# Second product of four gated MLPs by seven half-size products per block pair, in a tuned two-block transformer kernel

## The chip, the cores and the metric

The kernel runs on one core of a Trainium2 chip. The metric is the device time of one execution in microseconds (us), median over runs. The core has a matrix engine (TensorE, "PE" in the profile, its weight loads "PEld"), three elementwise engines (VectorE "DVE", ScalarE "ACT", GpSimd "POOL") and a queue of DMA issues (SyncE, "SP"). TensorE writes to 8 banks of PSUM, of 512 fp32 columns each; all else lies in one SBUF arena.

## The reference

512 tokens of width 1024 go through two layers of a first block and then through a second block. Each layer of the first block is: gated MLP, a mixer of three attentions, gated MLP. The change is about the four gated MLPs (`ffn1` and `ffn2` of both layers), and a little about two of the attentions:

```python
def swiglu(x, wg, wu, wd):                       # wg, wu: 1024 x 2816; wd: 2816 x 1024
    return (jax.nn.silu(x @ wg) * (x @ wu)) @ wd

x = x + 0.5 * swiglu(rmsnorm(x, ffn1_norm[l]), ffn1_wg[l], ffn1_wu[l], ffn1_wd[l])
```

The second block (two more mixers and 16 experts) is not touched. Everything is fp32. Each large product is made as three products of rounded operands (fp32r): with x = xh + xl and w = wh + wl it is wh·xh + wh·xl + wl·xh.

## The kernel before, in words

Activations lie feature-major: 128 features on the partitions, 512 tokens along the row. `ffn` (L783) has two halves. In the first, 11 groups `g` of 256 inner rows each make gate and up: per group 2 matrices x 2 tiles of 128 rows x 8 chunks of the 1024 inputs x 3 products, 96 matmuls of 512 columns. VectorE multiplies the gate sums by the norm's factor, ScalarE applies silu, VectorE multiplies by the up sums; the result of each 128-row tile is split into a rounded part `hh` and a rest `hl`, both kept for all 22 tiles. In the second half, 4 blocks `dp` of 256 output columns run over all 22 tiles: 22 x 2 x 3 = 132 matmuls of 512 columns each into two banks. Then VectorE scales each bank, adds it to the residual `x`, and `norm_prep` (L723) prepares the next norm: the scaled row, its rest, its square, the sum of squares.

Weights come as jobs of up to 128 x 1024 fp32 (`weights`, L666): a DMA into one of four raw buffers, a cast to fp32r (`copy`, L646: ScalarE or VectorE), and a subtraction in place for the rest (`tt`, L654: VectorE or GpSimd). Both helpers leave the engine open.

No order is written out by hand: `Recorder` (L77) first collects all operations with their dependencies, `schedule` (L296) then places them one by one on five engines with a table of assumed costs (`duration`, L518), chooses the engine of an operation with alternatives, gives PSUM banks to the products, and `search` keeps the best of nine tries. `emit` issues the result; each engine runs its list in that order. So all instructions have the line of `emit`, L500, and are told apart by shape. In the attentions some operands have 96 partitions (three parts of 32: `cqk`, `QP`, `KP`) and a few 64.

## Time and profile before

| | |
|---|---|
| runs of the kernel before | 2968.25 us median of 3 (2966.52 to 2971.15) |
| the profiled execution | 2972.06 us, span of its instructions 2970.3 us |
| granted TensorE clock, mean | 0.993 |
| TensorE busy | 2894.5 us, 97% of the span, 14909 matmuls |
| VectorE busy | 1669.2 us, 56% |
| ScalarE busy | 634.0 us, 21% |
| GpSimd busy | 279.2 us, 9% |

In the trace a matmul's record is longer than its turn on the engine, since matmuls are pipelined; the time of one in a row is the distance between two starts, or a stretch divided by its count. "Idle before" names what ended an engine's idle time. The arena is one tensor, so operations are named by their shape, and "bank" is PSUM.

### The profile page before, as it was taken

Reading aid. Unit: us, or ns where it says so; the run is one execution under the profiler, and the core shown is the slowest. Engines: PE = TensorE matmul, PEld = TensorE weight load, DVE = VectorE, ACT = ScalarE, POOL = GpSimd, SP = SyncE. Lnnn points to the kernel's source line nnn. Section 1 sums busy time; section 2 is a strip of 40 time slices with the busy share of each in tenths; the row PEclk is TensorE's granted clock in tenths of the full one; section 3 lists DMA queues with packets and bytes.
Section 4 is the critical chain, followed back from the end, with each engine's and each line's share of the span. In section 5 each row is a group of like instructions: output and inputs, shape, how many; then the busy total and the mean of one; then the engine's idle time right before and its main releaser. Section 6 shows DMA issues by size and latency. Waiting matters only on the chain.

```text
span 2970.3 us, 37457 instructions
## 1 busy us (share of the span) xinstructions
PE 2894.5 (97%) x14909; PEld 2192.1 (74%) x14909; DVE 1669.2 (56%) x3051; ACT 634.0 (21%) x1364; POOL 279.2 (9%) x279
## 2 busy tenths in 40 slices
PE   9999999999999999999999999999999999999998
PEld 7888877777888888888777778888777876444443
DVE  6554565886555455555658865555767783311212
ACT  3000133472000010001334721001222361100000
POOL 1000111211000010001112210000223120000000
PEclk9999999999999999999999999999999999999999
DMA  4333322102333333333221023333312356999999
GB/s 124 99 93 98 109 78 62 47 5 77 90 100 99 97 89 100 100 96 112 78 60 56 2 78 90 95 96 100 89 57 71 100 179 242 384 409 409 409 409 349
DMA packets 273139, 403.61 MB, mean 136 GB/s; under 512 B 34809, under 2 KB 210982, under 8 KB 272966
## 3 DMA queue, kind: packets, MB, share of 16 engines
q1 hardware_dynamic: 272806, 401.09, 40.1%
q8 instruction: 117, 1.92, 0.3%
q14 instruction: 56, 0.46, 0.0%
q0 software_dynamic: 160, 0.14, 0.0%
HBM read 399.09 MB, written 2.10 MB: 135 GB/s over the span
## 4 chain that ended last, share of the span: by engine, by line
PE 87%; DVE 8%; DMA 3%; issue 1%; ACT 1%; POOL 1%; SPq 0%; DVEq 0%; POOLq 0%; ACTq 0%
PE bank L500 87%; DVE arena L500 8%; DMA arena<-in_w_expert_up 1%; ACT arena L500 1%; DMA arena<-in_ffn_wd 1%; POOL arena L500 1%; DMA arena<-in_w_expert_down 0%; DMA arena<-in_x 0%; SPq L500 0%; DMA arena<-in_w_in 0%; DVEq L500 0%; DVEq L2189 0%; POOLq L500 0%; ACTq L500 0%
## 5 line engine op out<-in xcount | busy, mean ns | idle before, releaser
L500 PE MATMUL bank<-arena 128*128 128x512 f32 (+7 forms) x14909 | 2894.5, 383 | 71.7 <-DVE arena L500 40.5
L500 PEld LDWEIGHTS bank<-arena 128*128 128x128 f32 (+4 forms) x14681 | 2183.4, 176 | 751.9 <-issue 257.5
L500 DVE TENSOR_TENSOR arena<-arena 128x1024 fp32r<-128x1024 f32 (+11 forms) x889 | 689.5, 793 | 33.2 <-PE bank L500 9.1
L500 DVE CAST arena<-arena 128x1024 fp32r<-128x1024 f32 (+6 forms) x394 | 258.9, 658 | 629.4 <-PE bank L500 446.5
L500 POOL TENSOR_TENSOR arena<-arena 128x512 f32<-128x512 f32 (+13 forms) x159 | 206.6, 1306 | 1793.9 <-DVE arena L500 870.3
L500 ACT ACTIVATE arena<-arena 128x512 f32<-128x512 f32 (+4 forms) x313 | 189.2, 627 | 867.1 <-DVE arena L500 729.7
L500 ACT ACTIVATE arena<-bank,arena 128x256 f32<-128x256 f32 (+7 forms) x349 | 177.9, 534 | 452.5 <-PE bank L500 240.5
L500 DVE TENSOR_TENSOR arena<-arena,bank 128x512 f32<-128x512 f32 (+2 forms) x226 | 142.6, 668 | 103.4 <-PE bank L500 97.6
L500 ACT CAST arena<-arena 128x512 fp32r<-128x512 f32 (+3 forms) x94 | 74.5, 798 | 510.6 <-DVE arena L500 424.6
L500 ACT COPY arena<-bank 128x512 f32<-128x512 f32 (+5 forms) x194 | 102.8, 542 | 329.4 <-PE bank L500 324.6
L500 DVE TENSOR_TENSOR arena<-bank,arena 128x512 f32<-128x512 f32 (+3 forms) x207 | 135.2, 676 | 67.1 <-PE bank L500 50.0
L500 DVE SCALAR_TENSOR_TENSOR arena<-bank,arena 128x512 fp32r<-128x512 f32 (+5 forms) x71 | 46.6, 662 | 166.7 <-ACT arena L500 84.7
L500 DVE TENSOR_REDUCE arena<-bank 128x1 f32<-128x256 f32 (+3 forms) x208 | 97.5, 482 | 30.4 <-PE bank L500 27.2
L500 DVE TENSOR_SCALAR arena<-bank,arena 128x128 f32<-128x128 f32 (+5 forms) x88 | 32.4, 411 | 124.7 <-PE bank L500 124.4
L500 DVE TENSOR_SCALAR arena<-arena 128x512 f32<-128x512 f32 (+13 forms) x260 | 87.5, 358 | 17.4 <-ACT arena L500 12.3
L500 DVE COPY arena<-bank 128x512 f32<-128x512 f32 (+8 forms) x91 | 46.7, 514 | 85.2 <-PE bank L500 84.4
L500 DVE SCALAR_TENSOR_TENSOR arena<-arena 128x512 fp32r<-128x512 f32 (+8 forms) x162 | 86.5, 538 | 7.0 <-DMA arena<-in_attn_k_norm_w 4.3
L500 POOL TENSOR_SCALAR arena<-arena 128x512 f32<-128x512 f32 (+3 forms) x93 | 61.9, 668 | 295.2 <-DVE arena L500 259.7
L500 ACT CAST arena<-bank 128x512 fp32r<-128x512 f32 (+2 forms) x99 | 56.0, 577 | 94.8 <-PE bank L500 81.4
L500 ACT ACTIVATION_READ_ACCUMULATOR arena<-bank,arena 128x1 f32 x208 | 42.7, 205 | 0.0
L500 DVE RECIPROCAL arena<-arena 128x1 f32<-128x1 f32 (+2 forms) x249 | 38.0, 162 | 5.6 <-ACT arena L500 4.7
L500 PEld LDWEIGHTS <-arena 128*128 128x128 bf16 x228 | 21.4, 99 | 21.9 <-issue 15.1
(32 smaller groups left out, 157.6 us busy)
## 6 DMA issues: line engine op xcount, KB each, us to landing
arena<-in_w_expert_gate SPq DMA_DIRECT2D x64, 1024.0 KB
arena<-in_w_expert_up SPq DMA_DIRECT2D x64, 1024.0 KB
arena<-in_w_expert_down SPq DMA_DIRECT2D x62, 1024.0 KB
arena<-in_ffn_wg SPq DMA_DIRECT2D x88, 512.0 KB
arena<-in_ffn_wu SPq DMA_DIRECT2D x88, 512.0 KB
arena<-in_ffn_wd SPq DMA_DIRECT2D x80, 512.0 KB
arena<-in_w_in SPq DMA_DIRECT2D x36, 512.0 KB
arena<-in_w_in SPq DMA_DIRECT2D x32, 256.0 KB
```

Of the source, the lines that this page charges most:

```text
L500: last[i] = getattr(getattr(self.real, eng), m)(*a, **k).ins
```

## The change

The second product of each MLP is done by Strassen's scheme on blocks of 2 x 2: two tiles of inner rows times two tiles of output columns on the weights' side, two tiles of inner rows times two halves of the tokens on the activations' side. Where one pair of inner tiles and one column block took 12 matmuls of 512 columns, it now takes 7 products x 3 = 21 of 256 columns. For this

- `forms_b` replaces the split of a group's two tiles: 4 sums of 256 columns, and 7 forms (three plain, four sums) each with a rounded part and a rest;
- `forms_a` replaces `weights` for the second product's jobs: 4 sums of 256, then 7 forms with rounded part and rest, 1792 columns where there were 1024;
- `down` accumulates the seven products in four banks, and VectorE joins them by one copy and seven sums of 256 columns per column block; the scaling and the sum into `x` may now be done by GpSimd too;
- the inner rows are run in two chunks, groups 0 to 5 and 6 to 10, since all forms at once would not fit: six buffers for the activations' forms. So `x` is added to twice, and only the second chunk is followed by `norm_prep`.

In the attentions, operands of 96 or 64 partitions get 128, and GpSimd writes zeros into the rest (`blank`), once per buffer: 24 writes in all.

```diff
     def ffn(self, js, next_gain):
...
-                for f in range(2):
-                    t = hp.tile([128, T], F32, name="ht", tag="ht", bufs=3)
-                    h, lo = hh[:, 2 * g + f, :], hl[:, 2 * g + f, :]
-                    nc.vector.tensor_mul(t, ps[0][f], R)
-                    nc.scalar.activation(t, t, AF.Silu)
-                    nc.vector.tensor_mul(t, t, ps[1][f])
-                    self.copy(h, t)
-                    self.tt("tensor_sub", lo, t, f32(h))
...
-            for dp in range(4):
-                pds = [mmt() for _ in range(2)]
-                for gi, (f0, f1) in enumerate(self.fgs):
-                    wh, wl = self.weights(js["d"][dp][gi])
-                    for d in range(2):
-                        for f in range(f0, f1):
-                            self.mm3(pds[d], wh[:, f - f0, 128 * d:128 * d + 128], wl[:, f - f0, 128 * d:128 * d + 128],
-                                     hh[:, f, :], hl[:, f, :], f == 0, f == NF - 1)
...
+    CHUNKS = ((0, 6), (6, 11))
...
+                    B[g] = self.forms_b(hp, *ht)
+                if c:
+                    self.norm_end()
+                    self.norm2_begin() if next_gain == "two" else self.norm_begin(next_gain)
+                for dp in range(4):
+                    self.down(hp, mmt, js["d"][c][dp], B, g0, g1, dp, Rh)
+                    if c:
+                        for d in range(2):
+                            self.norm_prep(2 * dp + d)
+
+    def forms_b(self, hp, b1, b2):
...
+        hi, lo = (hp.tile([128, 7, 256], F32R, name=n, bufs=6) for n in ("bh", "bl"))
+        t = f32(lo[:, 3:7])
+        b11, b12, b21, b22 = b1[:, :256], b1[:, 256:], b2[:, :256], b2[:, 256:]
+        for n, (op, x, y) in enumerate((("tensor_sub", b12, b11), ("tensor_sub", b22, t[:, 0]), ("tensor_sub", b22, b12),
+                                        ("tensor_sub", t[:, 1], b21))):
+            self.tt(op, t[:, n], x, y)
+        w = lambda x: x.rearrange("p a b -> p (a b)")
+        for i, j, x in ((0, 1, b11), (1, 3, b2), (3, 7, w(t))):
+            h, o = w(hi[:, i:j]), w(lo[:, i:j])
+            self.copy(h, x)
+            self.tt("tensor_sub", o, x, f32(h))
+        return hi, lo
+
+    def forms_a(self, hp, j):
...
+        s = hp.tile([128, 1024], F32, name="sa", bufs=2)[:, :na * 512].rearrange("p (s a c) -> p s a c", s=4, a=na)
+        hi = hp.tile([128, 1792], F32R, name="ah", bufs=2)[:, :na * 896].rearrange("p (s a c) -> p s a c", s=7, a=na)
+        a11, a12, a21, a22 = v[:, :, 0, 0], v[:, :, 1, 0], v[:, :, 0, 1], v[:, :, 1, 1]
+        for i, (op, x, y) in enumerate((("tensor_add", a21, a22), ("tensor_sub", s[:, 0], a11), ("tensor_sub", a11, a21),
+                                        ("tensor_sub", a12, s[:, 1]))):
+            self.tt(op, s[:, i], x, y)
...
+        for h, x in ((hi[:, 0], a11), (hi[:, 1], a12), (hi[:, 2], a22), (w(hi[:, 3:7]), w(s))):
+            self.copy(h, x)
+            self.tt("tensor_sub", r32(x), x, f32(h))
...
+    def down(self, hp, mmt, jobs, B, g0, g1, dp, Rh):
...
+        ps = [mmt().rearrange("p (a b) -> p a b", a=2) for _ in range(4)]
+        for ga, gb, j in jobs:
+            ah, al = self.forms_a(hp, j)
+            for g in range(ga, gb):
+                bh, bl = B[g]
+                for m, n, q, e in self.PRODUCTS:
+                    w = ((ah, bh), (ah, bl), (al, bh))
+                    for i, (x, y) in enumerate(w):
+                        nc.tensor.matmul(ps[q][:, e], x(m, g - ga), y[:, n], start=g == g0 and i == 0 and e == 0,
+                                         stop=g == g1 - 1 and i == 2, skip_group_check=True)
+        (p1, p2), (p6, p7), (p5, p3), (p4, _) = [(p[:, 0], p[:, 1]) for p in ps]
...
+        self.copy(c1, p1)
+        nc.vector.tensor_add(y1[:, :256], c1, p2)
+        nc.vector.tensor_add(u2, c1, p6)
+        nc.vector.tensor_add(u3, u2, p7)
+        nc.vector.tensor_add(y1[:, 256:], u2, p5)
+        nc.vector.tensor_add(y1[:, 256:], y1[:, 256:], p3)
+        nc.vector.tensor_add(y2[:, 256:], u3, p5)
+        nc.vector.tensor_sub(y2[:, :256], u3, p4)
+        for d, y in enumerate((y1, y2)):
+            x = self.x[:, 2 * dp + d, :]
+            self.tt("tensor_mul", y, y, Rh)
+            self.tt("tensor_add", x, x, y)
...
-        KP = ap.tile([96, T], F32R, name="KP")
-        self.copy(KP, self.tr4(lambda c: self.three(hl[:, c]), pp))
+        KP = ap.tile([128, T], F32R, name="KP")
+        self.blank(KP, 96)
+        self.copy(KP[:96], self.tr4(lambda c: self.three(hl[:, c]), pp))
```

What the planner makes of it stands in the engines' lists. On TensorE, in the first MLP's second half, the list of before has products of 512 columns into two banks (arena_145 and arena_146 are the rounded part and the rest of the activations, arena_132 and arena_133 those of a job of weights):

```order
L500 MATMUL bank4_62<-arena_145,arena_132 128x512
L500 MATMUL bank2_60<-arena_146,arena_132 128x512
L500 MATMUL bank4_62<-arena_146,arena_132 128x512
L500 MATMUL bank2_60<-arena_145,arena_133 128x512
L500 MATMUL bank4_62<-arena_145,arena_133 128x512
```

Of the change, the start of the second chunk, behind the last gate and up products (arena_105 and arena_106 are the MLP's input, arena_147 and 148 the forms of a group's activations, arena_173 and 174 those of a job of weights):

```order
L500 MATMUL bank1_59<-arena_105,arena_130 128x512
L500 MATMUL bank1_59<-arena_106,arena_130 128x512
L500 MATMUL bank1_59<-arena_105,arena_135 128x512
L500 MATMUL bank5_63<-arena_147,arena_173 128x256
L500 MATMUL bank2_60<-arena_147,arena_173 128x256
L500 MATMUL bank4_62<-arena_147,arena_173 128x256
L500 MATMUL bank4_62<-arena_148,arena_173 128x256
L500 MATMUL bank4_62<-arena_147,arena_174 128x256
```

From there 420 products of 256 columns follow one another with none of 512 between them; in the first chunk the fourth column block alone is mixed with the next groups' gate and up products.

On VectorE, before, one column block's end and the weights of the next (arena_91 is `x`, 103, 105 and 106 the next norm's, 130 to 137 weights):

```order
L500 TENSOR_TENSOR arena_144<-bank1_59,arena_149 128x512
L500 TENSOR_TENSOR arena_147<-bank6_64,arena_149 128x512
L500 TENSOR_TENSOR arena_91<-arena_91,arena_144 128x512
L500 TENSOR_TENSOR arena_91<-arena_91,arena_147 128x512
L500 TENSOR_SCALAR arena_105<-arena_91,arena_98 128x512
L500 SCALAR_TENSOR_TENSOR arena_106<-arena_91,arena_98,arena_105 128x512
L500 CAST arena_132<-arena_136 128x1024
```

Of the change, at the same kind of place in the second chunk (arena_171 and 175 are the weights' sums, 177 and 178 forms, 179, 143 and 144 what is joined from the banks):

```order
L500 CAST arena_177<-arena_134 128x256
L500 CAST arena_173<-arena_132 128x256
L500 TENSOR_TENSOR arena_178<-arena_175,arena_177 128x1024
L500 TENSOR_TENSOR arena_135<-arena_134,arena_177 128x2x128
L500 TENSOR_TENSOR arena_179<-arena_179,bank0_58 128x256
L500 TENSOR_TENSOR arena_143<-arena_179,bank3_61 128x256
L500 TENSOR_TENSOR arena_135<-arena_134,arena_177 128x2x128
L500 TENSOR_TENSOR arena_143<-arena_179,bank5_63 128x256
L500 TENSOR_TENSOR arena_179<-arena_179,bank0_58 128x256
L500 TENSOR_TENSOR arena_171<-arena_124 128x128
```

The sums of banks and the forms of later jobs now stand between one another on one list. On GpSimd, before, these rows (the last is the mixer's) and one more sum into arena_103 and into `x` each are its arithmetic in the first MLP:

```order
L500 TENSOR_TENSOR arena_146<-arena_147,arena_145 128x512
L500 TENSOR_TENSOR arena_91<-arena_91,arena_147 128x512
L500 TENSOR_TENSOR arena_103<-arena_103,arena_107 128x512
L500 TENSOR_TENSOR arena_103<-arena_103,arena_108 128x512
L500 TENSOR_TENSOR arena_103<-arena_103,arena_107 128x512
L500 TENSOR_TENSOR arena_178<-arena_171,arena_177 128x576
```

Of the change, in the second chunk alone, 39 such operations, of which the first are:

```order
L500 TENSOR_TENSOR arena_166<-arena_143,arena_165 128x256
L500 TENSOR_TENSOR arena_171<-arena_171,arena_132 128x128
L500 TENSOR_TENSOR arena_171<-arena_132 128x128
L500 TENSOR_TENSOR arena_133<-arena_132,arena_173 128x128
L500 TENSOR_TENSOR arena_171<-arena_132,arena_171 128x128
L500 TENSOR_TENSOR arena_133<-arena_132,arena_173 128x128
L500 TENSOR_TENSOR arena_171<-arena_124 128x256
L500 TENSOR_TENSOR arena_135<-arena_134,arena_177 128x2x128 x2
```

GpSimd has taken over sums and rests that the weights' forms need, with 15 operations of 256 columns, 15 of 128 and 9 of 512 in that chunk.

## Rows read from the trace of the kernel before

**Rows 1.** The page, its first part: busy time by engine.
```profile
PE 2894.5 (97%) x14909; PEld 2192.1 (74%) x14909; DVE 1669.2 (56%) x3051; ACT 634.0 (21%) x1364; POOL 279.2 (9%) x279
```
**Rows 2.** The chain that ended last: start us, us, what, count.
```profile
PE 87%; DVE 8%; DMA 3%; issue 1%; ACT 1%; POOL 1%; SPq 0%; DVEq 0%; POOLq 0%; ACTq 0%
...
734.61 361.38 PE bank L500 x1600
```
**Rows 3.** Busy time by stretch: MLP groups and second product; the latter alone.
```profile
core 0: us, PE busy (x) PEld busy (x) DVE busy (x) ACT busy (x) POOL busy (x), PEclk, DMA share, GB/s
...
255.00:375.00 120.00, 118.96 (x524) 97.84 (x523) 62.16 (x73) 10.62 (x16) 11.39 (x7) 1.00 0.36 106
900.00:1060.00 160.00, 160.00 (x707) 132.18 (x706) 82.12 (x103) 9.70 (x16) 6.77 (x5) 1.00 0.31 96
```
**Rows 4.** Waits in the stretch 900 to 1060 us: who, for whom, us, times, longest.
```profile
DVE arena L500 <- PE bank L500: 66.4, 28, 7.0
```
**Rows 5.** Timeline of TensorE: first products of 256 columns, in two windows.
```profile
527.85 0.86 PE L500 MATMUL bank<-arena 128*128 128x256 f32 x5 [0.64 <-DVE arena L500]
...
527.85 0.62 PE L500 MATMUL bank<-arena 128*128 128x256 f32 x3 [0.64 <-DVE arena L500]
```
**Rows 6.** TensorE groups by shape: count, busy us, mean ns, idle before.
```profile
L500 PE MATMUL bank<-arena 128*128 128x512 f32 x8620 | 2060.9, 396 | 15.2 <-DVE arena L500 9.6 <-ACT arena L500 5.4
L500 PE MATMUL bank<-arena 128*128 128x256 f32 x312 | 57.0, 315 | 6.8 <-DVE arena L500 6.8
...
L500 PE MATMUL bank<-arena 128*128 128x384 f32 x96 | 28.4, 377 | 4.8 <-ACT arena L500 4.6
L500 PE MATMUL bank<-arena 96*128 96x512 f32 x28 | 12.1, 462 | 0.0
...
L500 PE MATMUL bank<-arena 96*128 96x384 f32 x28 | 11.4, 415 | 0.0
```
**Rows 7.** VectorE groups by shape, whole span.
```profile
L500 DVE TENSOR_TENSOR arena<-arena 128x1024 fp32r<-128x1024 f32 x332 | 412.9, 1244 | 8.6
L500 DVE CAST arena<-arena 128x1024 fp32r<-128x1024 f32 x303 | 217.5, 718 | 599.0 <-PE bank L500 419.9 <-DMA arena<-in_ffn_wg 99.1 <-DMA arena<-in_ffn_wu 61.9
...
L500 DVE TENSOR_TENSOR arena<-bank,arena 128x512 f32<-128x512 f32 x136 | 88.6, 686 | 46.2 <-PE bank L500 45.8
L500 DVE TENSOR_TENSOR arena<-arena 128x512 fp32r<-128x512 f32 x104 | 68.0, 686 | 0.6
...
L500 DVE CAST arena<-arena 128x512 fp32r<-128x512 f32 x63 | 26.9, 426 | 7.7 <-PE bank L500 5.9
```
**Rows 8.** Timelines, VectorE and GpSimd: a GpSimd sum alone; operations of VectorE alone.
```profile
983.85 1.29 POOL L500 TENSOR_TENSOR arena<-arena 128x512 f32<-128x512 f32 x1 [243.63 <-issue]
...
1012.42 0.49 DVE L500 TENSOR_SCALAR arena<-arena 128x512 fp32r<-128x512 f32 x1
1012.82 0.74 DVE L500 SCALAR_TENSOR_TENSOR arena<-arena 128x512 fp32r<-128x512 f32 x1
```
**Rows 9.** The same engines at work side by side, 20 to 25.6 us.
```profile
20.69 3.48 DVE L500 SCALAR_TENSOR_TENSOR arena<-arena 128x512 fp32r<-128x512 f32 x2
24.09 1.51 DVE L500 TENSOR_SCALAR arena<-arena 128x512 fp32r<-128x512 f32 x1
...
19.98 5.33 POOL L500 TENSOR_TENSOR arena<-arena 128x512 f32<-128x512 f32 x3 [2.99 <-ACT arena L500]
```
**Rows 10.** VectorE beside a GpSimd sum of 512 columns, 690.75 to 692.7 us.
```profile
691.44 0.68 DVE L500 TENSOR_TENSOR arena<-arena,bank 128x512 f32<-128x512 f32 x1
692.03 0.92 DVE L500 TENSOR_TENSOR arena<-arena 128x256 fp32r<-128x256 f32 x1
```
**Rows 11.** GpSimd groups by shape: the write nearest to the new ones.
```profile
L500 POOL CAST arena<-arena 128x896 fp32r<-128x896 f32 x2 | 2.4, 1220 | 10.8 <-PE bank L500 10.8
```

More of the change, by code (lines that the diff above doesn't have):

```diff
@@ L814, in ffn @@
[L814 to L831 removed]
+            R = Rh = None
@@ new lines, in ffn @@
+            B = {}
+            for c, (g0, g1) in enumerate(self.CHUNKS):
+                for g in range(g0, g1):
+                    ps = [[mmt() for _ in range(2)] for _ in range(2)]
+                    for m, h, j in js["gu"][g]:
+                        wh, wl = self.weights(j)
+                        for f in range(2):
+                            for k in range(4):
+                                self.mm3(ps[m][f], wh[:, k, 128 * f:128 * f + 128], wl[:, k, 128 * f:128 * f + 128],
+                                         xh[:, 4 * h + k, :], xl[:, 4 * h + k, :], h + k == 0, 4 * h + k == KC - 1)
+                    if g == 0:
+                        sm = lambda: pp.tile([128, T], F32, name="sm", bufs=2)
+                        R, Rh = (hp.tile([128, T], F32, name=n) for n in ("rrow", "rhalf"))
+                        r = self.norm_col(sm())
+                        self.copy(R, self.row_bcast(sm(), r))
+                        nc.vector.tensor_scalar_mul(Rh, R, 0.5)
+                    ht = []
+                    for f in range(2):
+                        t = hp.tile([128, T], F32, name="ht", tag="ht", bufs=4)
+                        nc.vector.tensor_mul(t, ps[0][f], R)
+                        nc.scalar.activation(t, t, AF.Silu)
+                        nc.vector.tensor_mul(t, t, ps[1][f])
+                        ht.append(t)
+                    B[g] = self.forms_b(hp, *ht)
+                if c:
+                    self.norm_end()
+                    self.norm2_begin() if next_gain == "two" else self.norm_begin(next_gain)
+                for dp in range(4):
+                    self.down(hp, mmt, js["d"][c][dp], B, g0, g1, dp, Rh)
+                    if c:
+                        for d in range(2):
+                            self.norm_prep(2 * dp + d)
@@ new lines, in forms_a @@
+    def forms_a(self, hp, j):
+        src, nk, n = self.jobs[j]
+        assert j == self.loaded
+        self.loaded += 1
+        na = nk // 2
+        raw = self.wp.tile([128, 1024], F32, name="raw", tag="raw", bufs=self.RAW)[:, :nk * n]
+        self.nc.sync.dma_start(raw.rearrange("p (k c) -> p k c", k=nk), src)
+        v = raw.rearrange("p (a f d c) -> p a f d c", a=na, f=2, d=2)
+        s = hp.tile([128, 1024], F32, name="sa", bufs=2)[:, :na * 512].rearrange("p (s a c) -> p s a c", s=4, a=na)
[4 more added lines that the diff above has]
+            self.tt(op, s[:, i], x, y)
+        w = lambda x: x.rearrange("p s a c -> p (s a c)")
+        for h, x in ((hi[:, 0], a11), (hi[:, 1], a12), (hi[:, 2], a22), (w(hi[:, 3:7]), w(s))):
+            self.copy(h, x)
+            self.tt("tensor_sub", r32(x), x, f32(h))
+        lows = [a11, a12, a22] + [s[:, i] for i in range(4)]
+        return (lambda m, i: hi[:, m, i]), (lambda m, i: r32(lows[m][:, i]))
@@ L1017, in tr4, with blank @@
         return ps[:r]
+    def blank(self, t, a):
+        self.nc.gpsimd.tensor_copy(t[a:], self.zero[a:].to_broadcast([128 - a, t.shape[1]]))
     def three(self, x):
@@ L1121, in mla_prep @@
         self.copy(w2h, w2)
-        self.tt("tensor_sub", w2l, w2[:64], f32(w2h[:64]))
+        self.tt("tensor_sub", w2l[:64], w2[:64], f32(w2h[:64]))
+        self.blank(w2l, 64)
         sc = 96 ** -0.5
@@ L1187, in mla_heads @@
             for n, (a, x) in enumerate((("w1h", "c1h"), ("w1h", "c1l"), ("w1l", "c1h"), ("w2h", "c2"), ("w2l", "c2"))):
[L1188 removed]
+                mm(ps, w(a), e[x], start=n == 0, stop=n == 4)
             Q = [self.stack2(mp, ps, x, "Q", 2, sc) for x in range(2)]
@@ L1245, in diff_heads @@
                     for s in range(2):
-                        t = mp.tile([96, T], F32R, name="cqk", bufs=8)
-                        self.copy(t, self.tr4(lambda tb: self.three(hl[s][:, tb, 2 * h + c]), pp))
+                        t = mp.tile([128, T], F32R, name="cqk", bufs=8)
+                        if p == 0:
+                            self.blank(t, 96)
+                        self.copy(t[:96], self.tr4(lambda tb: self.three(hl[s][:, tb, 2 * h + c]), pp))
                         qk.append(t)
```

61 lines of the change are left out of this document (22 added, 39 removed).

## The prediction

> **What bounds the kernel now.** I read the page's busy shares first: TensorE works 97% of the span, VectorE 56%, GpSimd 9% [rows 1]. The chain of waits puts 87% of the span on TensorE, and one of its pieces, 361.38 us with 1600 matmuls, runs without a break through an MLP [rows 2]. The busy time by stretch then shows the MLPs: from 900 to 1060 us TensorE is busy for all of 160.00 us with 707 matmuls, 226.3 ns each, while VectorE has 82 us of work and GpSimd 7; in a second product alone VectorE has 62 of 120 us [rows 3]. VectorE waits there for TensorE, 66.4 us in 28 waits [rows 4]. So a matmul less is time less, as long as the others stay ahead. They have half their time to spare, and the question is whether that holds when their work in the second product more than doubles.
>
> **TensorE's part.** Per MLP, 528 matmuls of 512 columns go: 528 x 226.3 ns = 119.5 us [rows 3]. In come 11 pairs of inner tiles x 4 column blocks x 21 = 924 of 256 columns. The first row of such products in the trace has 5 in 0.86 us and 3 in 0.62 us from the same start, so two more cost 0.24 us, 120 ns each [rows 5]. 924 x 120 ns = 110.9 us: **-8.6 us per MLP**. The bounds: half of 226.3, 113 ns, would give -14.9; the group's busy time over its count, 57.0 us / 312 = 183 ns, +49.6 [rows 6]. That group is mixed with other shapes and starts behind waits, so I take 120.
>
> The Trainium skill (page "TensorE: Matmul & The Clock Gate", section "Back-to-back issue gap") gives a matmul's spacing at full clock as columns/2.4 + 2.5 ns, 215.8 ns for 512 and 109.2 for 256; by it 12 x 215.8 - 21 x 109.2 = 296 ns would go per pair and block, an estimate of 52 us for the four MLPs instead of 34. The trace does not agree: 226.3 ns at 512.
>
> **VectorE's prices.** A sum or rest of 1024 columns is 412.9 us / 332 = 1.24 us, one of 512 is 68.0 / 104 = 0.65, and 88.6 / 136 = 0.65 from a bank [rows 7]. No undisturbed row has 256 or 128 columns; on the straight line through the two they are 0.36 and 0.21. That is my value; half of 0.65 and 0.65 itself are the ends for 256. A cast of 1024 is 217.5 / 303 = 0.72, of 512 0.43 [rows 7]; a scaled rest of 512 is 0.74 [rows 8].
>
> **The second chunk** has 20 pair-blocks, 420 x 0.12 = 50.4 us of TensorE, with no other product between them. What stands beside it:
> - weights' forms: 8 jobs of 7 x 0.36 + 1.24 = 3.76 and 4 half jobs of 7 x 0.21 + 0.65 = 2.12, together 38.6 us;
> - casts of the sums, by the lists 6 of 1024 and 3 of 512 on VectorE: 5.6 (the other casts are ScalarE's, which is 9% busy here [rows 3]; I cost them at nothing);
> - joining the banks, 4 x 7 x 0.36 = 10.1;
> - scaling and adding, 16 x 0.65 = 10.4;
> - the next norm, 8 x 0.74 + 7 x 0.65 = 10.5;
> - the last group's activation forms, 4 x 0.36 + 0.36 + 0.65 + 1.24 = 3.7.
>
> That is 78.9 us. Two jobs are formed ahead, under the last gate and up products (-9.0), and the last block's end lies under the mixer's first products, as it does before (-7.9): 62.0. Of this the lists give GpSimd 9 operations of 512, 15 of 256 and 15 of 128, at VectorE's prices 14.4. VectorE keeps **47.6 us**, just under the 50.4.
>
> What does GpSimd's help cost? Its sum of 512 takes 1.29 us alone [rows 8]. Side by side, VectorE needs 4.91 us (20.69 to 25.60) for two scaled rests and one scaling that alone take 2 x 0.74 + 0.49 = 1.97 [rows 8, 9], while GpSimd does three such sums: each holds VectorE up by 0.98 us. An operation that reads a bank goes on undisturbed (0.68 us), the next, of 256 columns from SBUF, takes 0.92 [rows 10]. Scaled by columns the 39 operations cost VectorE 9 x 0.98 + 15 x 0.49 + 15 x 0.25 = 19.9 us if all meet. A fifth of its own time reads banks (10.1 of 47.6), so four fifths meet: 15.7. 47.6 + 15.7 = 63.3, 12.9 over TensorE's 50.4. Ends: none meets, 47.6, nothing lost (0); all meet, 67.5, +17.1; each of GpSimd's operations adds its whole 1.29 us per 512 columns, 26.1 in all, 73.7, +23.3. I take **+15**, between the second and third value, because both lists are fixed and the four sums of a job hang on one another across the two engines, which the sum of prices does not hold.
>
> The Trainium skill (page "SBUF — State Buffer", section "Who interferes with whom") says that a VectorE operation with two SBUF inputs and a GpSimd operation that reads SBUF take turns, the second waiting for the whole of the first. By it the second chunk would end near the upper bound, +23. The trace agrees in kind (0.92 us against 0.68 in rows 10), and falls short of it in size (0.98 us per sum against 1.29).
>
> **The first chunk** has per block 15.1 us of TensorE and 3 x 3.76 + 2 x 0.72 + 2.5 + 2.6 = 17.8 of the others. The first three blocks: 53.4, less 9.0 formed ahead and 5.1 of the third's end, plus the fourth's first job 4.5, is 43.8 against 45.4. GpSimd's operations there (17 of 256, 6 of 512) add about 2. The fourth block is mixed with gate and up products, beside which VectorE has the slack of rows 4. So **+2**, ends 0 and +6. In the gate and up groups the forms (about 5 us a group instead of 2) hide under 96 x 226.3 ns = 21.7 us; where the cover fails, they cost the 3.
>
> **The attentions.** A matmul of 96 rows and 512 columns takes 12.1 us / 28 = 0.43 of busy time against 0.24 of a full one, at 384 columns 0.41 against 0.30 [rows 6]: 28 x 0.19 + 28 x 0.11 = 8.5 us for all. The narrower forms may bring as much again; half of such an excess may only be the next matmul's start. **-8**, ends 0 and -17. The 24 blank writes, a 512-column one some 0.7 us by the 1.22 for 896 [rows 11], lie on an idle GpSimd; uncovered they cost 17.
>
> **The sum.** Per MLP -8.6 + 15 + 2 = +8.4; four times +33.6; with the attentions +26. The profiled execution took 2972.06 us and would take 2998; the median of the runs is 3.8 lower, 2968.25, so I predict **2994 us**.
>
> **The rivals.** *The cover holds (faster).* If GpSimd's operations mostly fall where VectorE waits or reads banks, VectorE's 47.6 us stay under 50.4, and all of TensorE's gain comes: 4 x -8.6 - 8 = -42, 2926 us. For it: VectorE's waits in rows 4. Against it: rows 9, and that 62.0 us of vector work over 50.4 leave no waits. It decides once the two chunks lose less than 10 us an MLP. Chance 0.25. *A shorter pace too (faster).* 113 ns a product with the cover: 4 x -14.9 - 8, 2901 us; 0.03, since rows 5 speak against it. This is the direction of the page's spacing rule. *They cancel.* Two chunks lose 9 to 12 us an MLP: within 0.2% of 2968, 6 us, about what a measurement of this kernel can tell from no change. 0.09. *The long pace (slower).* If weight loads hold the new products to 183 ns, 924 x 63 ns = 58 us per MLP come on top, 4 x (49.6 + 2) - 8, some 3166 us, TensorE itself being the bound; 0.05. The forecast, 10 to 85 us slower, has 0.58. That the new products are not there at all is excluded by the lists.
>
> **The numbers.** The low end is the cover's case, 2924. The high end takes the worst bounds, 4 x (-8.6 + 23.3 + 6) = +83 and little from the attentions, 3056. The forecast's own range is 2975 to 3056. Faster by over 0.2%: 0.28; within: 0.09; slower: 0.63.
>
> **What would show it.** Products of 256 columns 120 ns apart where TensorE doesn't wait. TensorE's idle time before them put down to VectorE or GpSimd, most in the second chunk, 10 to 20 us an MLP, and hardly any under gate and up products. VectorE's sums of 256 columns at a mean well over 0.4 us, GpSimd busy over 400 us. Wrong it would be if TensorE's work in the second chunk took about 50 us from first product to last, or if its idle time lay in the first chunk; then the turns of the two engines cost less, or lie elsewhere, than said.

## The result, and the profile after

The changed kernel takes **3125.49 us** (median; 3123.26 to 3128.97), the kernel before 2968.77 beside it: a ratio of 1.0529 [1.0511, 1.0547], **157 us slower**. The forecast was 2994, 26 us slower, with a high end of 3056. The direction was right and the size six times too small. The profiled execution of the change took 3127.0 us.

The page's busy shares and its chain, to be held against [rows 1, 2]:

```profile
PE 2934.9 (94%) x16493; PEld 2289.8 (73%) x16493; DVE 2114.3 (68%) x3790; ACT 814.8 (26%) x1752; POOL 757.6 (24%) x720
...
PE 67%; DVE 21%; issue 4%; DMA 3%; POOL 3%; ACT 1%; SPq 0%; DVEq 0%; POOLq 0%; ACTq 0%
```

Span minus TensorE's busy time gives a ledger. The span grew by 155.0 us (2970.3 to 3125.3). TensorE's idle time grew from 75.8 to 190.4 us (+114.6). Its busy time grew too, from 2894.5 to 2934.9 (+40.4), although the arithmetic has 34 us less for it to do. So some 75 us went into products that ran longer. Experiment 4 gives a second measure: the same number and shape of products have TensorE busy for 2870.0 us there, 64.9 less. The waits of TensorE, first of the kernel before, then of the change (us, times, longest), name who was late:

```profile
PE bank L500 <- DVE arena L500: 40.5, 55, 2.6
```
```profile
PE bank L500 <- DVE arena L500: 151.0, 134, 3.4
```

It is mostly VectorE: 110.5 us more of the 114.6, in many waits of at most 3.4 us each. The busy time by stretch shows where. These are first and second chunks of the second products, cut from the first product of 256 columns to the last (MLPs 1 and 3 of the four; the sum is over all eight chunks):

```profile
core 0: us, PE busy (x) PEld busy (x) DVE busy (x) ACT busy (x) POOL busy (x), PEclk, DMA share, GB/s
154.60:238.80 84.20, 72.30 (x507) 68.17 (x506) 73.62 (x117) 14.54 (x30) 37.40 (x34) 0.92 0.26 82
345.80:418.30 72.50, 60.13 (x420) 57.49 (x419) 69.01 (x109) 21.36 (x48) 50.29 (x46) 0.88 0.22 66
...
1274.40:1359.10 84.70, 72.59 (x507) 68.79 (x506) 73.22 (x117) 14.55 (x30) 37.39 (x34) 0.92 0.26 81
1466.30:1538.90 72.60, 58.42 (x421) 55.12 (x420) 69.27 (x109) 21.15 (x48) 50.57 (x46) 0.93 0.22 66
...
sum 624.20, PE 528.54 PEld 499.62 DVE 573.51 ACT 150.95 POOL 345.59; mean PE 66.07 PEld 62.45 DVE 71.69 ACT 18.87 POOL 43.20
```

Before, a second product stood at a granted clock of 1.00 with VectorE half idle [rows 3]. Now VectorE is busy for 69.3 of 72.6 us in a second chunk, and 420 products that need 50.4 us take 72.6. The eight chunks hold 94.2 us of TensorE's waits: 11.6, 12.2, 11.5, 11.8, 12.0, 14.2, 12.3 and 8.6 us. The granted clock there is 0.88 to 0.96. The timeline of the first chunk of MLP 3 shows how VectorE falls behind (start us, us, what; in brackets the idle time before and who ended it):

```profile
1269.25 13.19 PE L500 MATMUL bank<-arena 128*128 128x512 f32 x88 [0.86 <-DVE arena L500]
...
1272.37 1.68 DVE L500 TENSOR_TENSOR arena<-arena 128x256 fp32r<-128x256 f32 x4
...
1277.59 6.07 POOL L500 TENSOR_TENSOR arena<-arena 128x256 fp32r<-128x256 f32 x7 [0.47 <-PE bank L500]
...
1278.56 5.72 DVE L500 TENSOR_TENSOR arena<-arena 128x256 fp32r<-128x256 f32 x7
...
1285.06 0.50 PE L500 MATMUL bank<-arena 128*128 128x256 f32 x2 [2.62 <-DVE arena L500]
...
1287.33 2.93 PE L500 MATMUL bank<-arena 128*128 128x256 f32 x12 [1.77 <-DVE arena L500]
```

At 1272 us four sums and rests of 256 columns take VectorE 1.68 us, 0.42 each, and GpSimd is silent. The row at 1278 merges unlike operations: beside GpSimd's seven (0.87 us each), VectorE has five of 256 columns, 0.76 to 0.96 us each, and one of 512, 1.22 us; its seventh, behind GpSimd's last, takes 0.41 again. Three of VectorE's and two of GpSimd's, one by one:

```profile
1279.11 0.80 POOL L500 TENSOR_TENSOR arena<-arena 128x256 f32<-128x256 f32 x1
1279.24 0.95 DVE L500 TENSOR_TENSOR arena<-arena 128x256 f32<-128x256 f32 x1
...
1279.99 0.80 POOL L500 TENSOR_TENSOR arena<-arena 128x256 f32<-128x256 f32 x1
1280.11 1.22 DVE L500 TENSOR_TENSOR arena<-arena 128x512 fp32r<-128x512 f32 x1
...
1283.87 0.41 DVE L500 TENSOR_TENSOR arena<-arena 128x256 f32<-128x256 f32 x1
```

GpSimd's first ends at 1279.91 and VectorE's beside it at 1280.19, 0.28 us later; the one of 512 columns ends 0.55 us after GpSimd's second. So VectorE does most of its operation only when GpSimd's is over: the two engines take turns. This is no chance of one place. In this trace 248 VectorE operations of 256 columns with both operands in SBUF began beside a running one of GpSimd, and 229 of them ended 0.28 us after it; 84 with an operand in a bank took 0.409 us in the same company. Over the whole span the VectorE groups of 256 columns show the same (count, busy us, mean ns), with GpSimd's below them:

```profile
L500 DVE TENSOR_TENSOR arena<-arena 128x256 f32<-128x256 f32 x321 | 218.6, 702 | 4.2 <-PE bank L500 1.5 <-POOL arena L500 0.6
...
L500 DVE TENSOR_TENSOR arena<-arena 128x256 fp32r<-128x256 f32 x181 | 104.5, 579 | 8.7 <-ACT arena L500 6.0 <-POOL arena L500 1.9
L500 DVE TENSOR_TENSOR arena<-arena,bank 128x256 f32<-128x256 f32 x232 | 87.2, 411 | 40.3 <-PE bank L500 29.4 <-ACT arena L500 10.5
```
```profile
L500 POOL TENSOR_TENSOR arena<-arena 128x256 f32<-128x256 f32 x189 | 177.8, 950 | 771.6 <-DVE arena L500 727.8 <-PE bank L500 37.5 <-issue 4.0
L500 POOL TENSOR_TENSOR arena<-arena 128x256 fp32r<-128x256 f32 x111 | 131.2, 1185 | 142.9 <-ACT arena L500 104.1 <-DVE arena L500 31.4 <-issue 4.8
```

An operation with one operand in a bank takes 0.411 us whoever is beside it; one with both operands in SBUF takes 0.70 on average.

Behind such waits TensorE's clock can be lower. The stretches around the two waits of 1285 and 1287 us, with the granted clock as the third number from the end of each row:

```profile
1282.00:1287.00 5.00, 0.94 (x6) 0.54 (x5) 4.86 (x7) 0.17 (x1) 1.66 (x2) 0.91 0.34 105
1287.00:1290.00 3.00, 2.67 (x12) 2.67 (x13) 2.86 (x7) 0.41 (x1) 0.73 (x1) 0.50 0.00 0
1290.00:1297.00 7.00, 7.00 (x50) 7.00 (x49) 4.58 (x8) 0.86 (x3) 1.84 (x3) 0.79 0.12 36
```

From 1282 to 1287 TensorE is busy for 0.94 of 5.00 us. Then the clock is at 0.50, the lower of its two levels (1.2 of 2.4 GHz), and 12 products take 2.67 us, 222 ns each instead of 120.

### The profile page after: what moved, and what is told of

It reads as the page before. It is cut to its first block, busy times and chain, and to the rows that moved or that the text cites. A ratio compares the mean times of both kernels' runs of the same rounds, so it can differ in the third digit from the quotient of the medians.

```text
span 3125.3 us, 42900 instructions
## 1 busy us (share of the span) xinstructions
PE 2934.9 (94%) x16493; PEld 2289.8 (73%) x16493; DVE 2114.3 (68%) x3790; ACT 814.8 (26%) x1752; POOL 757.6 (24%) x720
## 4 chain that ended last, share of the span: by engine, by line
PE 67%; DVE 21%; issue 4%; DMA 3%; POOL 3%; ACT 1%; SPq 0%; DVEq 0%; POOLq 0%; ACTq 0%
PE bank L500 67%; DVE arena L500 21%; POOL arena L500 3%; ACT arena L500 1%; DMA arena<-in_w_expert_up 1%; DMA arena<-in_w_expert_down 1%; DMA arena<-in_w_in 0%; DMA arena<-in_ffn_wu 0%; DMA arena<-in_x 0%; DMA arena<-in_nsa_phi_k 0%; DMA arena<-in_c_causal 0%; SPq L500 0%; DMA arena<-in_diff_lq 0%; DVEq L500 0%; POOLq L500 0%
## 5 line engine op out<-in xcount | busy, mean ns | idle before, releaser
L500 PE MATMUL bank<-arena 128*128 128x512 f32 (+8 forms) x16493 | 2934.9, 364 | 186.2 <-DVE arena L500 151.0
L500 PEld LDWEIGHTS bank<-arena 128*128 128x128 f32 (+2 forms) x16265 | 2281.2, 181 | 810.9 <-issue 256.0
L500 DVE TENSOR_TENSOR arena<-arena 128x256 f32<-128x256 f32 (+12 forms) x1449 | 1096.2, 790 | 51.6 <-ACT arena L500 18.1
L500 POOL TENSOR_TENSOR arena<-arena 128x256 f32<-128x256 f32 (+11 forms) x587 | 672.7, 1159 | 1455.1 <-DVE arena L500 1095.1
L500 ACT CAST arena<-arena 128x256 fp32r<-128x256 f32 (+4 forms) x432 | 237.2, 566 | 863.1 <-DVE arena L500 570.4
L500 ACT ACTIVATE arena<-arena 128x512 f32<-128x512 f32 (+2 forms) x341 | 205.6, 630 | 472.5 <-DVE arena L500 424.9
L500 DVE TENSOR_TENSOR arena<-arena,bank 128x256 f32<-128x256 f32 (+2 forms) x450 | 227.1, 540 | 137.2 <-PE bank L500 120.4
L500 ACT ACTIVATE arena<-bank,arena 128x256 f32<-128x256 f32 (+6 forms) x350 | 177.8, 531 | 468.2 <-PE bank L500 236.7
L500 ACT COPY arena<-bank 128x512 f32<-128x512 f32 (+3 forms) x213 | 110.1, 526 | 334.6 <-PE bank L500 331.3
L500 DVE TENSOR_TENSOR arena<-bank,arena 128x512 f32<-128x512 f32 (+4 forms) x175 | 113.8, 673 | 35.1 <-PE bank L500 16.3
L500 DVE RECIPROCAL arena<-arena 128x1 f32<-128x1 f32 (+2 forms) x249 | 38.4, 162 | 7.0 <-ACT arena L500 5.9
```

What stands on the lines that cost most here:

```text
L500: last[i] = getattr(getattr(self.real, eng), m)(*a, **k).ins
```

## The experiments

**1 and 2. Each half alone.** First the 128-row operands of the attentions, with the MLPs as before:

```diff
-        KP = ap.tile([96, T], F32R, name="KP")
-        self.copy(KP, self.tr4(lambda c: self.three(hl[:, c]), pp))
+        KP = ap.tile([128, T], F32R, name="KP")
+        self.blank(KP, 96)
+        self.copy(KP[:96], self.tr4(lambda c: self.three(hl[:, c]), pp))
...
```

> The 128-row operands alone, the MLPs as before. The prediction's term says 8 us faster, 2961. A rival, from the changed kernel's trace: its two mixers take 6 to 7 us longer each than before, so the wider operands with their blank writes cost, and this run is slower, about 2981. A second rival says the operands do nothing and the mixers' loss comes over from the MLPs: within 6 us of 2969.

Measured: 2966.81 us against 2969.06, ratio 0.9995 [0.9986, 1.0004]: no difference, as the last of the three expectations has it. TensorE's busy sum is 7.9 us lower in the profiled execution (2894.5 to 2886.6), which looks like the 8 of the prediction. But the two executions compared are 7.6 us apart by themselves (spans of 2970.3 and 2962.7 us), which their medians are not, and the products of the kernel before, put in another order, have a busy sum of 2883.2 (experiment 6). So the sum shows no gain, and why none came stays open. The blanks on GpSimd cost nothing that shows.

Then the seven products alone, with the attentions' lines turned back:

```diff
-        KP = ap.tile([128, T], F32R, name="KP")
-        self.blank(KP, 96)
-        self.copy(KP[:96], self.tr4(lambda c: self.three(hl[:, c]), pp))
+        KP = ap.tile([96, T], F32R, name="KP")
+        self.copy(KP, self.tr4(lambda c: self.three(hl[:, c]), pp))
...
```

> The second products by seven half-size products alone, attentions as before. If the 128-row operands gain 8 us, this run takes 3133; if they cost 13, 3112. In both cases over 140 us slower than before: the loss is the MLPs'.

Measured: 3105.07 us, 1.0458 [1.0444, 1.0472], under both expected values. The MLPs alone lose 136 of the 157 us. That the two halves together are 20 us worse than this one, though the other half is worth nothing, is most likely the planner: a changed operation anywhere gives other lists of the engines everywhere. No run shows it directly. If so, a difference of some 20 us between two of these kernels says little by itself.

**3. The weights' sums on VectorE alone.** In the forming of the weights and in the scaling and adding of the output, GpSimd is no longer offered the work; the activations' forms stay open to both.

```diff
+    def vt(self, op, out, a, b):
+        self.nc.put([[("vector", op, (out, a, b), {})]])
...
-            self.tt(op, s[:, i], x, y)
+            self.vt(op, s[:, i], x, y)
...
-            self.tt("tensor_sub", r32(x), x, f32(h))
+            self.vt("tensor_sub", r32(x), x, f32(h))
...
-            self.tt("tensor_mul", y, y, Rh)
-            self.tt("tensor_add", x, x, y)
+            self.vt("tensor_mul", y, y, Rh)
+            self.vt("tensor_add", x, x, y)
```

> The changed kernel, but the sums, rests, scaling and adding of the weights' forms and of the joins may go to VectorE only; the activations' forms stay open. Leaves no computation out. Theory 1, turns of VectorE and GpSimd: VectorE then has 62 us of work in the second chunk, where it now takes 72.5, and the first chunk loses its turns too: 8 to 18 us per MLP less, 3055 to 3095. Theory 2, the chain of four sums, cast and rest with two buffers sets the pace: fewer hand-overs between engines but more work on one, 3110 to 3150.

Measured: 3032.34 us, 1.0212 [1.0198, 1.0226], so 93 us of the 157 are gone, more than the first theory's range has. The two chunks of MLP 3 by stretch; VectorE's groups within the first of them; and, in the third fence, the same groups in the first chunk of the change (1274.40 to 1359.10 us):

```profile
1221.00:1289.10 68.10, 65.48 (x508) 63.23 (x507) 66.51 (x135) 19.46 (x40) 4.94 (x4) 1.00 0.31 101
1396.40:1461.30 64.90, 54.38 (x419) 52.91 (x419) 64.11 (x132) 21.81 (x49) 23.16 (x12) 0.95 0.27 87
```
```profile
L500 DVE TENSOR_TENSOR arena<-arena 128x256 f32<-128x256 f32 x42 | 19.4, 496 | 0.6 <-PE bank L500 0.5
L500 DVE TENSOR_TENSOR arena<-arena 128x1024 fp32r<-128x1024 f32 x14 | 17.1, 1218 | 0.0
L500 DVE TENSOR_TENSOR arena<-arena 128x256 fp32r<-128x256 f32 x32 | 13.5, 427 | 0.1
```
```profile
L500 DVE TENSOR_TENSOR arena<-arena 128x1024 fp32r<-128x1024 f32 x15 | 20.6, 1382 | 0.2
L500 DVE TENSOR_TENSOR arena<-arena 128x256 f32<-128x256 f32 x29 | 20.1, 719 | 0.6 <-PE bank L500 0.4
...
L500 DVE TENSOR_TENSOR arena<-arena 128x256 fp32r<-128x256 f32 x23 | 13.1, 572 | 1.4 <-ACT arena L500 0.7 <-POOL arena L500 0.6
```

The first chunk has 135 VectorE operations in 66.5 us, where the change had 117 in 73.2. Giving GpSimd 30 operations more (34 instead of 4) made VectorE's own list 18 shorter and 6.7 us longer (ScalarE does 10 fewer there). With GpSimd nearly away the first chunk takes 68.1 us instead of 84.7, at clock 1.00 and with 2.6 us of waits. The second chunk is now bounded by VectorE, busy for 64.1 of 64.9 us.

What the turns cost VectorE can be estimated from the traces. Take each of its operations without an operand in a bank that has GpSimd beside it, and subtract the median that the same shape takes in the same trace with GpSimd silent. Over the eight chunks this gives 150 us in the change (15 of them on casts), 54 here and 22 in experiment 5. In MLP 3 it is 16.6 us in the first chunk and 20.7 in the second of the change, and 3.5 and 11.6 here: the 12 operations that GpSimd has left in the second chunk still hold VectorE up.

**4. Without the sums.** The four sums of each weight job, their casts and their rests are left out; the products read the plain blocks in their place, so the number and shape of the products stay.

```diff
-        for h, x in ((hi[:, 0], a11), (hi[:, 1], a12), (hi[:, 2], a22), (w(hi[:, 3:7]), w(s))):
+        for h, x in ((hi[:, 0], a11), (hi[:, 1], a12), (hi[:, 2], a22)):
...
-        lows = [a11, a12, a22] + [s[:, i] for i in range(4)]
+        lows = [a11, a12, a22, a11, a12, a22, a11]
+        hi = [hi[:, n % 3] for n in range(7)]
...
```

> Leaves out the four sums on the weights' side, with their casts and rests: the seven products use the three plain forms in their place, in the same number and size. Vector work per job falls from 3.8 us of sums and rests to about 1.1. If the vector side (turns or chain) is what is late, TensorE runs through and the time is 2926 to 2950. If the products of 256 columns, or a lower clock that does not come from waits, cost the time themselves, it stays above 3000.

Measured: 2965.3 us (one run), TensorE busy 2870.0. The second chunk of MLP 3 by stretch:

```profile
1363.10:1413.40 50.30, 50.30 (x420) 50.27 (x419) 43.22 (x95) 14.95 (x34) 15.44 (x15) 1.00 0.32 97
```

420 products run without a break at 119.8 ns each, so TensorE's gain is as predicted where its operands are ready. GpSimd still has 488 operations in this kernel, which do no harm while VectorE has time to spare (43.2 of 50.3 us). The rest of the 34 us didn't come: TensorE's idle time is 92.7 us instead of 75.8. Some of it stands at the ends of the second chunks (2.7 us behind those of MLPs 1 and 3); the rest was not followed. The bound of 2926 to 2950 was missed.

**5. A planner that knows of the turns.** Nothing of the kernel's work changes. The list builder gets one more rule: an operation of GpSimd, or one of VectorE that is a copy or a scaling or has two operands, with none in a bank, starts only when the last such operation has ended by its plan.

```diff
+                if shares(op, e) and turns > t:
+                    bank = None
+                    q.remove(i)
+                    heapq.heappush(p, (turns, i))
+                    continue
...
             end = t + d
+            if shares(op, e):
+                turns = end
```

> The changed kernel with nothing altered but the planner's idea of time: it now lets a VectorE operation with two SBUF operands and any GpSimd operation take turns, so it hands GpSimd work only where VectorE is not about to use the port. If the turns of the two engines are the main loss and the planner makes it by not knowing of them, the loss shrinks to about what the version with the weights' sums on VectorE alone has: 3020 to 3070 us, and the mean of a 256-column sum on VectorE falls from 0.70 us towards 0.54. If instead the two buffers of the weights' forms and the chain of four sums set the pace, whoever makes them, it stays at 3100 to 3140 us.

Measured: **2977.07 us**, 1.0022 [1.0013, 1.0032], 148 us less than the change, and better than expected. GpSimd is left with 325 operations of 720. The chunks of MLP 3 and the sum over all eight, and VectorE's sums of 256 columns over the span:

```profile
1200.00:1267.40 67.40, 65.27 (x502) 62.71 (x501) 64.20 (x136) 19.43 (x40) 4.12 (x4) 1.00 0.32 102
1373.60:1429.80 56.20, 52.27 (x420) 50.66 (x419) 55.95 (x123) 22.22 (x50) 14.59 (x15) 1.00 0.30 92
...
sum 498.50, PE 478.37 PEld 461.37 DVE 479.75 ACT 172.61 POOL 74.19; mean PE 59.80 PEld 57.67 DVE 59.97 ACT 21.58 POOL 9.27
```
```profile
L508 DVE TENSOR_TENSOR arena<-arena 128x256 f32<-128x256 f32 x463 | 189.0, 441 | 4.9 <-DMA arena<-in_ffn_wd 2.0 <-PE bank L508 1.2 <-issue 0.2
...
L508 DVE TENSOR_TENSOR arena<-arena 128x256 fp32r<-128x256 f32 x269 | 110.9, 421 | 2.2 <-ACT arena L508 2.0
```

0.44 and 0.42 us instead of 0.70 and 0.58, and both chunks stand at clock 1.00. But VectorE is still full: over the eight chunks it is busy for 479.8 of 498.5 us, and TensorE for 478.4, so 20.1 us are still lost there, with 22 us of turns left by the estimate of experiment 3.

**6. The control.** The same rule in the kernel before.

> The kernel before, planned with the turns of VectorE and GpSimd (the control for the version that took 2977 us). If the turns cost something only where the seven products made VectorE full, this is the kernel before: 2960 to 2970 us, and the seven products, so planned, stand at +7 to +17 us against it. If the rule also mends much of the rest of the kernel (the joints between MLPs and mixers, the mixers themselves), it falls to 2930 to 2955 us, and the version at 2977 us still hides a loss of 20 to 45 us in the MLPs.

Measured: **2952.56 us**, 0.9940 [0.9926, 0.9955], in the second of the expected ranges: the fastest of all, and faster than both kernels. GpSimd's busy time falls from 279.2 to 144.8 us. So some 16 of the 148 us have nothing to do with the seven products, which under this planner still cost 2977.07 - 2952.56 = 24.5 us.

**7. Only the first chunk by seven products**, sums and rests, scaling and adding on VectorE, the second chunk multiplied as before, attentions as before:

```diff
-                    B[g] = self.forms_b(hp, *ht)
+                    B[g] = self.plain_b(hp, *ht) if c else self.forms_b(hp, *ht)
...
-                    self.down(hp, mmt, js["d"][c][dp], B, g0, g1, dp, Rh)
+                    (self.plain if c else self.down)(hp, mmt, js["d"][c][dp], B, g0, g1, dp, Rh)
```

> The seven products in the first chunk alone (inner rows 0 to 5 of 11 pairs), with sums, rests, scaling and adding there on VectorE only; the second chunk is multiplied as before (240 matmuls of 512 columns, two banks), and the attentions are as before. If VectorE's work is what the second chunk lacks room for, and the first has room once GpSimd keeps out (68.2 us in that version), TensorE's gain of 6/11 x 8.6 = 4.7 us an MLP comes: 2969 - 19 = 2950 us, and up to 9 more (2959) where the joints take back 2.2 us an MLP as without the sums. If the split itself costs more than that (a joining of banks and a second adding of the output per MLP), the time is at or over the kernel before: 2963 to 2990 us.

Measured: 2995.53 us, 1.0087 [1.0072, 1.0102]; the 2950 didn't come. With the planner's rule and the sums open to both engines:

> The seven products in the first chunk only, attentions as before, sums and rests free for either engine, planned with the turns. The version without the rule took 2995 us, 26 over the kernel before, though its second product's second half is multiplied as before. If what it lost was again GpSimd's sums of the activations beside a full VectorE, the rule takes it to the gain of TensorE, 2945 to 2960 us. If it was the second joining and the unlike shapes around it, it stays at 2985 to 3000 us.

Measured: 2969.33 us, 1.0000 [0.9990, 1.0009], under neither expectation: 26 us less than without the rule, but 17 over the control. Its TensorE is busy for 2877.6 us, 5.6 less than the control's 2883.2 and not 19.

**8. Casts off VectorE.** As experiment 3, with the casts of the weights' forms on ScalarE alone.

```diff
-            self.copy(h, x)
+            self.nc.put([[("scalar", "copy", (h, x), {})]])
             self.vt("tensor_sub", r32(x), x, f32(h))
```

> The version with the weights' sums and rests on VectorE only, and beside that the casts of these forms on ScalarE only. If VectorE's own work is what still bounds the second chunk there (63.7 of 64.4 us busy), some 5.6 us of casts less on it shorten each second chunk by 4 to 5.6 us: 3032 - 16 to 22, so 3010 to 3017 us. If the buffers or the chain of sums bound it, the casts only change engine: 3026 to 3040 us, and VectorE has waits in the second chunk.

Measured: 3036.72 us, 1.0225 [1.0210, 1.0241]: no gain. In the second chunk of MLP 3 VectorE is still busy for 64.28 of 66.30 us:

```profile
1399.50:1465.80 66.30, 57.24 (x427) 55.02 (x427) 64.28 (x130) 30.30 (x62) 21.31 (x13) 0.91 0.28 86
```

VectorE's list there is as long as it was (130 operations, after 132), so the room went to other work. The time lies in the range of the theory that buffers are the bound, but VectorE has only 2.0 us of waits in that chunk, which speaks against it. The run decides neither.

**9. The seven products alone, under the rule, and with measured prices.** First without the attentions' part:

> The seven products alone (attentions as before), planned with the turns. The attentions came out at nothing by themselves, so 2970 to 2984 us, as with them; should the blanks on GpSimd, which the rule now puts in line with VectorE, cost there, 2955 to 2970 us.

Measured: 2976.36 us, 1.0024 [1.0015, 1.0034], the same as with it. Then with the planner's prices set to the measured ones:

```diff
-        return max(n / 2.4 + 2.5, 56.0 if st.dtype == BF else 107.0)
+        return max((n + 32) / 2.4, 56.0 if st.dtype == BF else 107.0)
...
-        return 68 + 1.042 * n
+        return 147 + 1.047 * n
...
-    return 126 + 2.123 * n
+    return 110 + 2.48 * n
```

> The seven products alone with the turns, and the planner's prices set to what the runs measured: a VectorE sum 147 ns + 1.047 ns a column (0.415 us at 256, 0.683 at 512) instead of 68 + 1.042, a GpSimd sum 110 + 2.48 a column, a matmul (columns + 32)/2.4. If too low a price of the short operations is what remains of the loss, 5 to 20 us less than without the prices: 2955 to 2970 us. If VectorE's own work is the limit of the second chunk (some 4 us over TensorE's 50.4 there), prices change nothing: within 5 us of the version without them.

Measured: 3022.16 us, 1.0177 [1.0162, 1.0192], 46 us worse. Truer prices gave a worse plan. Why wasn't found out; it shows how far lists of this planner scatter, and that the 93 us of experiment 3 and the 148 of experiment 5 are beyond that. The 20 of experiment 2, the 16 and 24.5 of experiment 6, the 26 of experiment 7 and the 13 of experiment 10 are not: what these are put down to rests on the traces, not on the times.

**10. Three MLPs.** What are the last 24 us? In experiment 5 TensorE is busy for 14.5 us less than in the control (2868.7 and 2883.2) and idle for 38.4 more (107.0 and 68.6). Of its idle time 20.1 us lie in the eight chunks, beside a full VectorE. The next piece is the end of the last MLP. The timeline of TensorE and the busy time at the end of the last MLP, first two fences of experiment 5, then two of the control:

```profile
2097.78 15.73 PE L508 MATMUL bank<-arena 128*128 128x256 f32 x126
2114.34 0.38 PE L508 MATMUL bank<-arena 128*128 128x256 f32 x1 [0.83 <-POOL arena L508]
2128.21 20.02 PE L508 MATMUL bank<-arena 128*128 128x512 f32 x80 [13.49 <-DVE arena L508]
```
```profile
2126.00:2147.00 21.00, 18.79 (x76) 15.90 (x77) 16.16 (x46) 7.98 (x12) 0.00 (x0) 0.76 0.08 25
```
```profile
2097.75 10.52 PE L508 MATMUL bank<-arena 128*128 128x512 f32 x48
2109.26 39.00 PE L508 MATMUL bank<-arena 128*128 128x512 f32 x201 [0.99 <-DVE arena L508]
```
```profile
2126.00:2147.00 21.00, 21.00 (x112) 18.12 (x111) 19.44 (x33) 11.12 (x16) 1.82 (x2) 1.00 0.34 101
```

By seven products the last output blocks come out of four banks at the very end, and their joins, scaling, adding and norm lie bare: TensorE waits 13.49 us, and runs at a mean clock of 0.76 behind it. By plain products it waits 0.99. So the last MLP was multiplied as before, with the attentions as before too:

```diff
-... self.ffn_jobs(l, 2)))
+... (self.ffn_jobs0 if l else self.ffn_jobs)(l, 2)))
...
-                self.ffn(f2, self.gain["ffn1_norm", 1] if l == 0 else "two")
+                (self.ffn0 if l else self.ffn)(f2, self.gain["ffn1_norm", 1] if l == 0 else "two")
```

> The seven products in the first three MLPs, the fourth multiplied as before; attentions as before; planned with the turns. The version with all four (2976 us) has a wait of 13.6 us for VectorE at the end of the fourth MLP, after the last joins, and 20.5 us of half clock behind it, some 10 us more. If that uncovered end is most of what keeps the seven products over the kernel before so planned (2953 us), it goes with them and the fourth MLP's gain of 8.6 us goes too: 2976 - 23 + 9 = 2962 us. If the loss is spread over all four MLPs, a quarter of it goes: 2967 to 2974 us. Only under 2950 us would the seven products be worth having.

Measured: **2963.03 us**, 0.9983 [0.9974, 0.9992], close to the 2962 that the bare end gives, and 13 us under the 2976.36 of experiment 9. It beats the kernel before by 0.2%, and not the control, by 10.5 us.

## Why the prediction was wrong

The mechanism came as forecast; the step that failed is its price, in the first chunk above all. The prediction gave the turns 15.7 + 2 us an MLP, and by the estimate of experiment 3 they took 20.7 + 16.6 in MLP 3. The clock and the ends of the chunks stand in its sum at nothing; what they cost by themselves was not separated. Term by term:

- **TensorE, -8.6 us an MLP: right.** 119.8 ns a product where nothing is waited for, 120 predicted from [rows 5]. The Trainium skill (page "TensorE: Matmul & The Clock Gate", section "Back-to-back issue gap"), by whose formula for an isolated product it would be 109.2 ns, does not agree with it.
- **The second chunk, +15: the place was right, the size too small.** It was 72.5 and 72.6 us in MLPs 1 and 3 and 67.2 in MLP 4, over 50.4: +17 to +22, so at the bounds of +17.1 and +23.3 that were named and not taken. VectorE was to have 63.3 us of work, 47.6 of its own and 15.7 of turns; it was busy for 69.0, 69.3 and 65.9. In MLP 3 the turns are 20.7 of the 69.3 us by the estimate of experiment 3, which leaves 48.6 of its own. So its own work was right, and the argument that only four fifths of GpSimd's operations meet VectorE's failed: with VectorE full, they all meet (19.9 us in the prediction's sum for that case). The Trainium skill (page "SBUF — State Buffer", section "Who interferes with whom") has the second of two such operations wait for the whole of the first; the 229 of 248 operations that ended 0.28 us behind GpSimd's agree. VectorE's busy time lies nearest to the 67.5 us of "all meet"; the stretch of 72.6 us, in which VectorE is idle for 3.3, lies nearest to 73.7. The kernel before shows the same turns: there 34 of 41 operations of 512 columns that began beside GpSimd's ended 0.55 us after it. They would have given the price of a meeting.
- **The first chunk, +2: the step that failed most.** It took 83 to 85 us where 68.1 is what the same products take with GpSimd away. The prediction added up work of both engines (43.8 us against 45.4) as if dividing it were free, and gave GpSimd's operations there 2 us more; the turns cost VectorE 16.6 there in MLP 3. The 52 sums and rests of 256 columns that VectorE has in that stretch of MLP 3 take 20.1 + 13.1 = 33.2 us instead of 52 x 0.36 = 18.7. Part of this is the price alone: the straight line through 512 and 1024 columns gave 0.36, and an undisturbed one takes 0.42. The larger part is the turns. They are not all of the stretch's loss: VectorE is also idle for 11.5 of its 84.7 us (1.6 of 68.1 in experiment 3), 6.7 of them put down to TensorE's banks, so the two wait for one another.
- **The clock: not in the sum.** Cover was costed as waits. But TensorE's busy time in the eight chunks is 528.5 us, and some 57 more than the same products have undisturbed (65.5 us a first chunk in experiment 3; 50.3 a second one in experiment 4, 58.8 where products of 512 lie among them). How much of it is a loss of its own is open: where VectorE is full, slow products fill time in which TensorE would else wait. Together with the 94 us of waits it covers what the chunks lost, 152.5 us over the 471.7 that their products take undisturbed. Less the 34 that TensorE gains this is 118 of the 155 us by which the span grew. The other 37 lie outside the chunks and were not followed; the mixer of the first layer takes 363.0 us for 357.0, with as many products.
- **Ends and joints: not in the sum.** The last block's end was taken as covered ("as it does before"). In the last MLP it isn't: 13.5 us of wait and a lower clock behind it in experiment 5.
- **The attentions, -8: wrong.** Nothing came, the end "0" of the range. The prediction held part of the excess of 96-row products to be only the next product's start; whether all of it was, no run shows.
- **The signs.** Products 120 ns apart, sums of 256 columns well over 0.4 us and GpSimd busy over 400 us (757.6) came true. That TensorE's waits lie mostly in the second chunks did not: the first chunks hold 47.4 of the 94.2 us, which the prediction had named as a sign of being wrong.
- **The rivals.** The cover did not hold, and the products did not run at 183 ns. The forecast had the right mechanism with 0.58, and its range was too narrow by 69 us, since its high end counted every bound of VectorE's work but neither the clock nor the first chunk's turns beyond 6 us.

That the turns are the main cause is shown from two sides: GpSimd kept off the weights' sums (-93 us), and GpSimd given work only where the plan has no such operation on VectorE (-148, of which 16 come without the seven products too). The time that VectorE loses to turns falls along with it, from 150 us to 54 and 22. That nothing is left of TensorE's 34 us even then is shown in part: 20.1 us beside a full VectorE in the chunks, and the bare end of the last MLP. Of the 10.5 us by which three MLPs by seven products stay behind the control, the cause was not looked for.

## What to carry to other kernels

A second engine that takes work off a full one is no help if the two take turns: count what the full engine's remaining operations will take beside it, not what it is relieved of. A gain on the bounding engine has to be weighed against the work that it puts on its supplier by stretch, and a supplier that just fits does not fit, for behind its small waits TensorE can run at the lower clock, so that a wait can cost twice. Where lists are made by a planner, put such a rule into the planner before judging a change by it: here the kernel that nobody had meant to change was 0.6% faster with the same rule, though another list alone may be worth that much.

## What the runs showed of the hardware

- VectorE's and GpSimd's sums with all operands in SBUF take turns: 229 of the 248 VectorE operations of 256 columns that began beside a running one of GpSimd ended 0.28 us after it, and took 0.76 to 0.96 us each where both had a row of them, against 0.42 for VectorE alone. VectorE's casts are held up too (15 of 150 us in the eight chunks). With an operand in a bank VectorE isn't held up: 0.409 us beside GpSimd, 0.411 over all in the change, 0.415 in experiment 3.
- Short operations have a fixed part: 0.41 us at 256 columns and 0.68 at 512 (with a bank), so about 0.15 us before the first column.
- Products of 256 columns: 119.8 ns; at the lower clock 222.
- Behind two waits of 2.62 and 1.77 us, close upon one another in an MLP, the granted clock was 0.50; behind the wait of 13.49 us a stretch of 21 us had a mean of 0.76.
